# The first stage of a one-core hybrid attention and LRU layer, written in another order

## The chip, the cores and the metric

The kernel runs on one core of one Trainium2 chip. The metric is device time in microseconds (us), the median of repeated runs. Five engines work side by side, each through a queue of its own in order: PE (TensorE, matmuls), DVE (VectorE), ACT (ScalarE), POOL (GpSimd) and SP (SyncE, which here only issues DMAs). An instruction that waits holds back everything behind it on its engine.

## What is computed

A sequence of 512 tokens with 2048 features passes through one layer. The part that matters here is its beginning:

```python
def rms_norm(x, w):
    xf = x.astype(jnp.float32)
    y = xf * lax.rsqrt(jnp.mean(xf * xf, axis=-1, keepdims=True) + EPS)
    return (y * w.astype(jnp.float32)).astype(x.dtype)
...
    h = rms_norm(x, norm_w)
    proj = jnp.einsum('bsd,de->bse', h, w_in)
    q, k, v, g_attn, xr, g_lru = jnp.split(proj, SPLITS, axis=-1)
    attn_out = attention_group(q, k, v, q_norm_w, k_norm_w)
    lru_out = lru_group(xr, conv_w, conv_b, lru_wa, lru_ba, lru_wx, lru_bx, lru_lambda)
    mixed = jnp.concatenate([rms_norm(attn_out, attn_norm_w) * jax.nn.silu(g_attn),
                             rms_norm(lru_out, lru_norm_w) * jax.nn.silu(g_lru)], axis=-1)
    return x + jnp.einsum('bse,ed->bsd', mixed, w_out)
```

The LRU group takes the 1024 columns xr of the projection, convolves each with four taps along the tokens, and sends the result through block-diagonal gates and a scan. Everything is float32.

## The kernel before

Every float32 product is made of three matmuls: each operand is split into a high part (an fp32r copy) and a low part (the rest), and PE adds high x high, high x low and low x high (`mm3`, L152 to L155). x and w_in are both loaded in eight chunks of 256 features, 512 KB each. A chunk of w_in for 512 columns is one tile `wr`, and `wsplit` (L220) splits each of its two halves: ACT copies it to `wh` (L227), DVE subtracts to get `wl` (L228). There are four buffers of `wh` and of `wl` at this time, so a split of a chunk waits until PE has used the chunk two before it; the ring for `wr` holds three chunks.

The first stage computes xr, whose two halves of 512 columns are `a1` (PSUM banks `pj`) and `a2` (banks `mm`). x must arrive transposed. Chunks 0 and 1 are turned on PE (`xturn`, L257). Chunks 2 to 7 are turned by way of DRAM: DVE transposes 32x32 blocks (`block_x`, L345, instructions at L290), SP writes the result to a DRAM tile `xd` in four DMAs (`aside_x`, L350, issued at L305), SP reads it back in one DMA as `xu` (`back_x`, L353, issued at L312), ACT multiplies by norm_w (L360) and copies the high part (L366), and DVE subtracts the low part (L367; the two together are `whole_x`, L356). The read back waits for all four writes.

Beside that, 1/rms is needed: the sums of squares of every chunk (`square_x`, L342: on DVE for chunks 0 and 1, L281; on ACT for the others, L277), their sum on DVE (`xsum`, L401), the power on POOL (`rsqrt_mean`, L371), four small DVE instructions and one of 128x512 that lays the values out on a diagonal (`rows`, L379; L385, L386, L388), a matmul with ones (L395) and a copy to `rbc` (L396). The projection is multiplied by `rbc` as it is taken out of PSUM (`evac_bc`, L502, and L1285 for the first bank).

PE's order is written by hand: chunks 0 and 1 of a1, chunks 0 and 1 of a2, chunks 2 to 7 of a1 with the matmul of L395 ahead of the last quarter of chunk 7, six quarter chunks of a2, and then the gates of LRU block 0 (`lru_pair`, L525, from L553 on), with more of a2 between the gates of the following blocks. Ahead of the gates of a block, DVE takes xr out of PSUM, ACT starts the convolution (`xc`, L535), DVE adds three taps (L540, three times), ACT copies the high part (L545) and DVE subtracts the low part (L546).

What ACT, DVE, SP and POOL do in the first stage, and in which order, is set by the table `moves` (L1244): at the step of PE's order that is its key, it lists what to do. A letter is an action (`acts`, L1239) and the digit a chunk: L loads x, B turns its blocks, D writes them to DRAM, R reads them back, V makes the two parts of x, Q squares; W loads weights of a1 and S splits them; F and P do so for a2; T and H are the turn on PE; C makes some steps of the LRU's constants (`lru_consts`, 16-column instructions on DVE, `lc`); Z is 1/rms. SP and POOL take the first stage's instructions in the written order; for ACT and DVE that holds up to step (6, 0), and from there a scheduler interleaves what is left with the LRU's work. `behind(held)` (L251) tells that scheduler to place an instruction after another one.

Of the kernel before, what the change touches and what calls it, by code (L numbers as in the profile page):

```python
# [63 lines left out]
def hybrid_kernel(  # L64
# [20 lines left out]
    nc = tc.nc  # L85
# [32 lines left out]
    def nm(s):  # L118
        cnt[0] += 1
        return f"{s}_{cnt[0]}"  # L120
# [25 lines left out]
    def const(shape, name, dt=F32):  # L146
        return cp.tile(list(shape), dt, tag=name, name=name)

    def f(ap):
        return ap.bitcast(F32)  # L150
# [55 lines left out]
    loads_done, held = {}, []  # L206

    def wraw(w, r0, c0, nk=1, queue=nc.sync):

        raw = wring.tile([P, 2, SEQ], F32, name=nm("wr"))  # L210
        src = w[r0 : r0 + 2 * P, c0 : c0 + SEQ].rearrange("(k p) e -> p k e", p=P)
        for k in range(nk):
            ks = slice(k * 2 // nk, (k + 1) * 2 // nk)
            with behind(held):
                loads_done[queue] = queue.dma_start(raw[:, ks, :], src[:, ks, :]).ins
            yield raw

# [2 lines left out]
    def wsplit(raw, k, copy=nc.scalar.copy):  # L220

        turn_of[0] += k
        pool = pools["wx" if "wx" in pools and turn_of[0] % 2 else "xw"]
        hi = pool.tile([P, SEQ], F32R, tag="wh", bufs=4, name=nm("wh"))
        lo = pool.tile([P, SEQ], F32R, tag="wl", bufs=4, name=nm("wl"))
        done = (
            copy(hi, raw[:, k, :]).ins,  # L227
            nc.vector.tensor_sub(lo, raw[:, k, :], f(hi)).ins,  # L228
        )
        split_done[-1] = split_done[turn_of[0] - k] = done  # L230
        return hi, lo

# [18 lines left out]
    def behind(those):  # L251
        stack = ExitStack()
        for ins in those:
            stack.enter_context(tc.issue_after(ins))
        return stack
# [71 lines left out]
    chunk, squares, halves, units, reads = {}, {}, {}, {}, []  # L327
# [38 lines left out]
            nc.scalar.copy(hi, v)  # L366
            nc.vector.tensor_sub(lo, v, f(hi))  # L367

    last_pool = [None]

    def rsqrt_mean(dst, src, n, width):  # L371

# [6 lines left out]
    def rows(dst, col, dg):  # L379

        shape = [P, NT, 2, P // 2]
        two = const([P, NT, 4], "two", F32R)[:, :, :2]
        for n in range(2):
            own, other = (slice(m * P // 2, (m + 1) * P // 2) for m in (n, 1 - n))
            nc.vector.tensor_copy(two[own, :, n], col[own])  # L385
            nc.vector.tensor_sub(two[other, :, n], col[own], f(two[own, :, n]))  # L386
        d = dg()
        nc.vector.tensor_mul(  # L388
            d.rearrange("p t (h q) -> p t h q", h=2),
            both_.rearrange("p (h q) -> p h q", h=2)[:, None].broadcast_to(shape),  # L390
            f(two)[:, :, :, None].broadcast_to(shape),
        )
        yield
        pb = pj()
        nc.tensor.matmul(pb, ones_r, d.rearrange("p t q -> p (t q)"), start=True, stop=True)  # L395
        nc.vector.tensor_copy(dst, pb)  # L396
        yield
# [480 lines left out]
    P1, Q6, Q5, Q7, P2, Q3, Q4 = 0, 5, 4, 3, 2, 6, 1  # L878
# [324 lines left out]
    with tc.high_priority():  # L1203
        xs, ws = xload(0, 2), wraw(w_in, 0, C_XR, 2)
        nc.scalar.dma_start(nw_st, norm_w.rearrange("(k p) -> k p", p=P))
        xc, raw = next(xs), next(ws)
# [28 lines left out]
    def vectors(_):  # L1235
# [6 lines left out]
        "C": lambda n: drain(itertools.islice(lrc, n)), "F": fetch_next, "P": split_next, "G": vectors,  # L1242
    }
    moves = {  # L1244
# [10 lines left out]
    }  # L1255

    def move(step):
# [5 lines left out]
    done = []  # L1263
# [22 lines left out]

    s1.close()
    s0.close()
    held.append(reads[-1])
    last_x = loads_done["lru"] = reads[-1]  # L1290
    wsums = itertools.chain(first_sums(), more_sums())

# [209 lines left out]
```

## Time and profile before

| | us |
|---|---|
| median of 3 runs | 628.86 |
| lowest, highest run | 628.76, 628.90 |
| profiled execution, device time | 629.26 |
| its span, first to last instruction | 627.3 |
| outside the span (the difference) | 1.96 |
| mean granted TensorE clock | 1.00 |

A row of a timeline shows the start and the duration in us, the engine and line, output and inputs, and in brackets the idle time of the engine before it with what ended it. "x2" is two instructions in one row; the duration is then that of both.

### The profile page before, as it was taken

How to read it: one execution, taken by the hardware profiler on the slowest of the kernel's cores; microseconds unless marked ns; L12 is line 12 of the kernel's file. 1: busy time of each engine (PE TensorE's matmuls, PEld its weight loads, DVE VectorE, ACT ScalarE, POOL GpSimd, SP SyncE). 2: the span in 40 equal slices, each digit the busy share in tenths (PEclk: the TensorE clock that was granted, in tenths of full speed). 3: DMA queues.
4: the chain of work that ended last, by engine and by line, in shares of the span. 5: the costliest groups of instructions: out<-in, count | busy, mean ns of one | idle time of the engine just before them, and what ended most of it. 6: DMA issues, size and time to landing. Idle time of an engine off the chain costs nothing.

```text
span 627.3 us, 8287 instructions
## 1 busy us (share of the span) xinstructions
PE 620.0 (99%) x2732; PEld 509.4 (81%) x2732; DVE 495.8 (79%) x789; ACT 360.8 (58%) x648; POOL 106.2 (17%) x142
## 2 busy tenths in 40 slices
PE   9999999999999999999999999999999999999997
PEld 7787788887888788888888888888888888888886
DVE  6577878997979896787787888549979866887776
ACT  4587589869946832645485547338346534433441
POOL 3001111112003442521123232100210101010010
PEclk9999999999999999999999999999999999999999
DMA  8996989557975589688669646932995776897262
GB/s 287 358 296 219 262 149 240 142 140 172 245 224 165 164 185 246 133 191 274 187 193 271 194 126 187 279 90 69 262 266 176 234 244 226 300 334 238 68 202 100
DMA packets 76218, 130.76 MB, mean 208 GB/s; under 512 B 6952, under 2 KB 31120, under 8 KB 76176
## 3 DMA queue, kind: packets, MB, share of 16 engines
q1 hardware_dynamic: 68064, 112.75, 57.6%
q0 software_dynamic: 7936, 17.36, 14.7%
q8 instruction: 21, 0.34, 0.2%
q14 instruction: 21, 0.17, 0.1%
q10 hardware_dynamic: 176, 0.14, 0.1%
HBM read 111.87 MB, written 39.32 MB: 241 GB/s over the span
## 4 chain that ended last, share of the span: by engine, by line
PE 79%; DVE 9%; DMA 5%; ACT 4%; issue 2%; SPq 1%; POOL 1%; DVEq 0%; ACTq 0%
PE pj L155 14%; PE pj L153 14%; PE pj L154 14%; PE mm L1065 14%; PE pj L1065 11%; PE mm L155 4%; PE mm L153 4%; PE mm L154 4%; DMA wr<-in_w_in_dram 2%; DVE wl L228 2%; DVE b L584 1%; DMA xu<-xd 1%; ACT wh L227 1%; DVE k L540 1%; DVE b L581 1%
## 5 line engine op out<-in xcount | busy, mean ns | idle before, releaser
L227 ACT CAST wh<-wr 128x512 fp32r<-128x512 f32 x142 | 84.3, 617 | 79.6 <-PE pj L154 32.0
L155 PE MATMUL pj<-x,wl 128*128 128x512 f32 x304 | 118.6, 390 | 0.6 <-DVE wl L228 0.6
L153 PE MATMUL pj<-x,wh 128*128 128x512 f32 x304 | 118.5, 390 | 0.6 <-ACT wh L227 0.6
L154 PE MATMUL pj<-x,wh 128*128 128x512 f32 x304 | 118.3, 389 | 0.0
L228 DVE TENSOR_TENSOR wl<-wr,wh 128x512 fp32r<-128x512 f32 x144 | 98.8, 713 | 17.7 <-ACT wh L227 16.3
L913 ACT CAST wh<-wr 128x1024 fp32r<-128x1024 f32 (+1 forms) x72 | 60.6, 860 | 75.2 <-PE mm L1065 35.4
L914 DVE TENSOR_TENSOR wl<-wr,wh 128x1024 fp32r<-128x1024 f32 (+1 forms) x72 | 68.5, 983 | 29.1 <-ACT wh L913 29.0
L154 PE MATMUL pj<-wl,x 128*128 128x512 f32 x192 | 75.0, 390 | 0.5 <-DVE wl L228 0.5
L153 PE MATMUL pj<-wh,x 128*128 128x512 f32 x192 | 74.9, 390 | 0.2 <-ACT ev L627 0.2
L155 PE MATMUL pj<-wh,x 128*128 128x512 f32 x192 | 74.8, 389 | 0.0
L155 PEld LDWEIGHTS pj<-x,wl 128*128 128x128 f32 x304 | 57.1, 188 | 13.8 <-DVE wl L228 1.9
L153 PEld LDWEIGHTS pj<-x,wh 128*128 128x128 f32 x304 | 57.1, 188 | 12.7 <-ACT wh L227 1.3
L154 PEld LDWEIGHTS pj<-x,wh 128*128 128x128 f32 x304 | 57.1, 188 | 11.8
L937 POOL DMA_DIRECT2D t<-in_w_out_dram x40 | 33.3, 896 | 137.8 <-DMA t<-in_w_out_dram 76.2
L1065 PE MATMUL mm<-wh,ml 128*128 128x512 f32 x126 | 49.0, 389 | 0.0
L1065 PE MATMUL mm<-wh,mh 128*128 128x512 f32 x126 | 49.0, 389 | 0.0
L1065 PE MATMUL mm<-wl,mh 128*128 128x512 f32 x126 | 49.0, 389 | 0.0
L154 PEld LDWEIGHTS pj<-wl,x 128*128 128x128 f32 x192 | 36.0, 188 | 8.6 <-DVE wl L228 1.2
L153 PEld LDWEIGHTS pj<-wh,x 128*128 128x128 f32 x192 | 36.0, 188 | 8.5 <-ACT ev L627 0.8
L155 PEld LDWEIGHTS pj<-wh,x 128*128 128x128 f32 x192 | 36.0, 188 | 7.4
L737 POOL TENSOR_SCALAR p<-p,sm 128x512 f32<-128x512 f32 x32 | 24.2, 759 | 89.8 <-DVE sm L736 89.8
L1065 PE MATMUL pj<-wl,mh 128*128 128x512 f32 (+1 forms) x100 | 38.5, 385 | 0.0
(229 smaller groups left out, 1171.9 us busy)
## 6 DMA issues: line engine op xcount, KB each, us to landing
wr<-in_w_in_dram SPq DMA_DIRECT2D x71, 512.0 KB, 5.1
wr<-in_w_out_dram SPq DMA_DIRECT2D x21, 512.0 KB, 5.9
t<-in_w_out_dram POOLq DMA_DIRECT2D x40, 256.0 KB, 7.4
wr<-t SPq DMA_DIRECT2D x40, 256.0 KB, 5.4
pd<-u SPq DMA_DIRECT2D x16, 512.0 KB, 3.0
pt<-pd SPq DMA_DIRECT2D x64, 128.0 KB, 3.9
t<-in_w_out_dram SPq DMA_DIRECT2D x24, 256.0 KB, 5.6
wr<-in_w_out_dram SPq DMA_DIRECT2D x22, 256.0 KB, 5.0
```

The lines of the kernel that those rows point to most:

```text
L153: nc.tensor.matmul(acc, lh, rh, start=start, stop=False)
L154: nc.tensor.matmul(acc, lh, rl, start=False, stop=False)
L155: nc.tensor.matmul(acc, ll, rh, start=False, stop=stop)
L227: copy(hi, raw[:, k, :]).ins,
L228: nc.vector.tensor_sub(lo, raw[:, k, :], f(hi)).ins,
L540: nc.vector.scalar_tensor_tensor(xc[:, d0:d1], xr[:, d0 + o : d1 + o], v1(R_CW + j * NB + n), xc[:, d0:d1], op0=ALU.mult, op1=ALU.add,)
L581: nc.vector.tensor_mul(i, i, t)
L737: last_pool[0] = nc.gpsimd.tensor_scalar(p, p, sm, 0.0, op0=ALU.mult, op1=ALU.add).ins
L913: nc.scalar.copy(hi[:, to], b)
L914: nc.vector.tensor_sub(lo[:, to], b, f(hi[:, to]))
L937: nc.gpsimd.dma_start(dst, src, accum_op=ALU.add)
L1065: nc.tensor.matmul(dst[s][:, es], lh[:, ts_], rh[:, es], start=i == ends_[0] and j == 0, stop=i == ends_[1] and j == 2,)
```

## The change

Only the first stage and one condition behind it are touched. The table `moves` is written in another order, and two small edits change what waits in the scheduler's order: the load of a later chunk of weights is placed after the last read back alone, and the split of such a chunk after the diagonal of 1/rms (`laid`).

```diff
-            with behind(held):
+            with behind(held[:1]):
                 loads_done[queue] = queue.dma_start(raw[:, ks, :], src[:, ks, :]).ins
...
-        done = (
-            copy(hi, raw[:, k, :]).ins,
-            nc.vector.tensor_sub(lo, raw[:, k, :], f(hi)).ins,
-        )
+        with behind(held[1:]):
+            done = (
+                copy(hi, raw[:, k, :]).ins,
+                nc.vector.tensor_sub(lo, raw[:, k, :], f(hi)).ins,
+            )
...
-        nc.vector.tensor_mul(
+        laid[0] = nc.vector.tensor_mul(
...
-        None: "G0 Q0 L1 W1 S1 L2 F0 L3 L4 F1 W2",
-        (0, 2): "T1 H1 H1 B2 D2 P0 B3 L5 D3 W3",
+        None: "G0 Q0 L1 W1 S1 L2 F0 L3",
+        (0, 2): "T1 H1 B2 H1 L4 D2 F1 W2 R2",
...
-        (6, 0): "V7 S7 Z0 Z0",
+        (6, 0): "V7 S7 Q7 Q4 Z0 Z0 C3",
...
-    held.append(reads[-1])
+    held.extend((reads[-1], laid[0]))
```

All lines from 226 on stand one line further down in the changed kernel. PE's order is the same in both.

On SP, at the beginning of the stage, this stands in the kernel before. `b4` is a chunk of x, `wr` one of weights, `xd` the write to DRAM and `xu` the read back.

```order
L248 DMA b4_28_219<-in_x_dram 128x4x256
L215 DMA wr_29_221<-in_w_in_dram 128x2x512
L215 DMA wr_30_223<-in_w_in_dram 128x2x512
L305 DMA xd_39_263<-xu_37_257 32x4x256 x4
L248 DMA b4_46_282<-in_x_dram 128x4x256
L305 DMA xd_47_284<-xu_44_276 32x4x256 x4
L215 DMA wr_48_289<-in_w_in_dram 128x2x512
L312 DMA xu_38_258<-xd_39_263 128x1024
```

And at the same place in the changed kernel:

```order
L249 DMA b4_36_257<-in_x_dram 128x4x256
L306 DMA xd_37_259<-xu_34_249 32x4x256 x4
L215 DMA wr_38_264<-in_w_in_dram 128x2x512
L215 DMA wr_39_266<-in_w_in_dram 128x2x512
L313 DMA xu_35_250<-xd_37_259 128x1024
L306 DMA xd_46_295<-xu_44_289 32x4x256 x4
```

The four writes of chunk 2 stand ahead of two chunks of weights, and its read back ahead of the load of chunk 5 and the writes of chunk 3.

On DVE, behind the diagonal of 1/rms, this stands before. `k2_124` is the diagonal, `ev` xr out of PSUM, `wl` a low part of weights.

```order
L388 TENSOR_TENSOR k2_124_725<-both_95,two_720 128x512
L396 COPY rbc_105<-pj_126_766 128x512
L502 TENSOR_TENSOR ev_131_789<-pj_11_169,rbc_105 128x512
L228 TENSOR_TENSOR wl_151_858<-wr_149_855,wh_150_857 128x512
L228 TENSOR_TENSOR wl_153_862<-wr_149_855,wh_152_861 128x512
L502 TENSOR_TENSOR ev_132_791<-pj_12_170,rbc_105 128x512
L1285 TENSOR_TENSOR ev_125_752<-ev_125_752,rbc_105 128x512
```

And in the changed kernel, where `lc` are the LRU's constants of 16 columns:

```order
L389 TENSOR_TENSOR k2_124_714<-both_95,two_709 128x512
L482 TENSOR_TENSOR lc4_567<-lc4_567,lc3_566 128x16
L229 TENSOR_TENSOR wl_146_824<-wr_144_821,wh_145_823 128x512
L483 TENSOR_SCALAR lc4_567<-lc4_567 128x16
L229 TENSOR_TENSOR wl_148_828<-wr_144_821,wh_147_827 128x512
L482 TENSOR_TENSOR lc4_567<-lc4_567,lc3_566 128x16
L397 COPY rbc_105<-pj_126_766 128x512
L483 TENSOR_SCALAR lc4_567<-lc4_567 128x16
L229 TENSOR_TENSOR wl_151_858<-wr_149_855,wh_150_857 128x512
L482 TENSOR_TENSOR lc4_567<-lc4_567,lc3_566 128x16
L229 TENSOR_TENSOR wl_153_862<-wr_149_855,wh_152_861 128x512
L483 TENSOR_SCALAR lc4_567<-lc4_567 128x16
```

The two splits of weights that stood ahead of the diagonal (`wl_146`, `wl_148`) now stand behind it, and the rest of the constants stands between the wide instructions. Up to `ev_125` there follow `k2_135`, `ev_131` and `ev_132` with five more `lc` and constants among them: nine wide and eleven small instructions from the diagonal to `ev_125`, where there were six wide ones.

On ACT, between the splits of two later chunks of weights, this stands before. `k2_136` is the beginning of the convolution of LRU block 0 (from `ev_125`), `k2_137` its high part.

```order
L227 CAST wh_150_857<-wr_149_855 128x512
L227 CAST wh_152_861<-wr_149_855 128x512
L530 CAST k2_134_795<-k2_127_777 128x512
L535 ACTIVATE k2_136_799<-ev_125_752,vec_102 128x512
L227 CAST wh_161_914<-wr_160_912 128x512
L227 CAST wh_163_918<-wr_160_912 128x512
L545 CAST k2_137_804<-k2_136_799 128x512
```

And in the changed kernel:

```order
L228 CAST wh_150_857<-wr_149_855 128x512
L228 CAST wh_152_861<-wr_149_855 128x512
L531 CAST k2_134_795<-k2_127_777 128x512
L228 CAST wh_161_914<-wr_160_912 128x512
L536 ACTIVATE k2_136_799<-ev_125_752,vec_102 128x512
L228 CAST wh_163_918<-wr_160_912 128x512
L546 CAST k2_137_804<-k2_136_799 128x512
```

The beginning of the convolution stands behind the first split of chunk 4 of a2 (`wh_161`) and no longer ahead of it. DVE's three taps stand behind the low part of the same split (`wl_162`) in the changed kernel, where two of the three stood ahead of it.

More of the change, by code (lines that the diff above doesn't have):

```diff
@@ L367, in whole_x @@
             nc.vector.tensor_sub(lo, v, f(hi))
-    last_pool = [None]
+    last_pool, laid = [None], [None]
     def rsqrt_mean(dst, src, n, width):
@@ L391, in rows @@
             f(two)[:, :, :, None].broadcast_to(shape),
-        )
+        ).ins
         yield
```

14 rows, old and new, of the table moves are left out of this document.

## The prediction

> **What bounds the kernel now.** The page comes first: PE is busy all along.
>
> ```profile
> span 627.3 us, 8287 instructions
> PE 620.0 (99%) x2732; PEld 509.4 (81%) x2732; DVE 495.8 (79%) x789; ACT 360.8 (58%) x648; POOL 106.2 (17%) x142
> ```
>
> 620.0 / 2732 is 0.227 us for a matmul. PE's order is not changed, so only its waits can go or come. PE's timeline over the first stage shows them: where a start follows the one before by more than 0.23 us, PE waited.
>
> ```profile
> 18.76 0.48 PE L153 MATMUL mm<-x,wh 128*128 128x512 f32 x1
> ...
> 29.54 0.39 PE L155 MATMUL mm<-x,wl 128*128 128x512 f32 x1
> 30.55 0.50 PE L153 MATMUL pj<-x,wh 128*128 128x512 f32 x1 [0.62 <-ACT wh L227]
> ...
> 64.46 0.47 PE L395 MATMUL pj<-k,ones_r 128*128 128x512 f32 x1 [0.76 <-DVE k L388]
> ...
> 74.54 0.40 PE L154 MATMUL pj<-k,k 128*128 128x512 f32 x1
> ```
>
> The windows view counts the matmuls between the first of these rows and L395 (the second row serves further down):
>
> ```profile
> 18.70:64.40 45.70, 43.80 (x188) 34.45 (x186) 30.04 (x85) 32.27 (x89) 1.60 (x2) 1.00 0.86 282
> 20.00:40.00 20.00, 19.22 (x84) 15.27 (x83) 12.90 (x34) 15.15 (x45) 0.00 (x0) 1.00 1.00 333
> ```
>
> 188 records touch the window; two began before it. 186 × 0.227 = 42.2 us out of 45.7: without a wait L395 would start at 61.0, so PE waits 3.5 us here: 0.8 at chunk 2 (29.54 to 30.55 less a matmul), 0.76 idle at the diagonal, the rest in short waits between them, which all end with the later one. L395 to the low-part gate matmul (74.54) is 10.08 us, 44 matmuls without a wait.
>
> **The path to chunk 2.** The chain of waits shows the path through DRAM, DVE's timeline what stood ahead of it, ACT's its landing.
>
> ```profile
> 15.13 0.34 SPq L305
> 16.00 3.44 DMA xd<-xu
> 20.60 6.99 DMA xu<-xd
> ```
>
> ```profile
> 11.11 1.29 DVE L228 TENSOR_TENSOR wl<-wr,wh 128x512 fp32r<-128x512 f32 x2 [0.26 <-ACT wh L227]
> ...
> 35.21 1.42 DVE L290 STREAM_TRANSPOSE xu<-b 128x256 f32<-128x256 f32 x4
> ```
>
> ```profile
> 27.61 1.34 ACT L360 ACTIVATE xu<-xu,nw 128x512 f32<-128x512 f32 x2 [4.85 <-DMA xu<-xd]
> 30.93 1.33 ACT L360 ACTIVATE xu<-xu,nw 128x512 f32<-128x512 f32 x2
> 43.54 1.34 ACT L360 ACTIVATE xu<-xu,nw 128x512 f32<-128x512 f32 x2 [2.68 <-DMA xu<-xd]
> ```
>
> The writes land at 19.4, yet the read is issued at 20.60, because on SP it stands behind the load of chunk 5, the writes of chunk 3 and a load of weights. In the new order it stands right behind its writes and two loads of weights. The blocks of chunk 2 now follow the first pair of low parts, which ends at 12.4, so writes and read go out 1.3 to 2 us sooner: read issued about 18.8. With 7.0 us for the landing as here, chunk 2 is there at 25.8; PE's first matmul of it came 2.94 us behind ACT's start (30.55 − 27.61), so 28.7, ahead of the 29.77 at which PE is free. The 0.8 us go. If DMA were no faster for it, nothing would go here, but what follows hangs on chunk 5 and not on this.
>
> **The path to L395: chunk 5 and the squares.** ACT has squares last now, so from chunk 5's landing on it works in one piece. How soon it lands: on SP its read stands behind the four writes of chunk 6, in both orders; these wait for the blocks of chunk 6 on DVE, and these stand behind chunk 3's parts, 4.28 us behind their start on ACT (35.21 − 30.93).
>
> ```profile
> 36.66 1.82 SPq L305 DMA_DIRECT2D xd<-xu  x4
> 38.53 0.46 SPq L312 DMA_DIRECT2D xu<-xd  x1
> ```
>
> ```profile
> DMA to landing us min/median/max: 5.0/5.8/7.0
> ```
>
> The last row is the source view of L312. Chunk 3's parts stood right behind chunk 2's (30.93 − 27.61 = 3.3); with chunk 2 at 25.8 they could start at 29.1, and I take 29.5, since chunk 3's read now waits for its own writes right ahead of it on SP. The same steps then give blocks from 33.8 to 35.2, writes of 1.82 and the read of chunk 5 at 37.1 instead of 38.53; with the shortest landing, which that read itself took (38.53 to 43.54), chunk 5 is there at T5 = 42.1. The bounds are 41.2 (chunk 3's parts at 29.1 and 0.5 us of the writes beside the blocks) and 43.5 (no gain). From T5 on:
>
> ```profile
> 49.97 1.32 ACT L360 ACTIVATE xu<-xu,nw 128x512 f32<-128x512 f32 x2
> ...
> 53.27 0.41 ACT L277 ACTIVATE b<-b 128x256 f32<-128x256 f32 x1
> ...
> 54.88 1.32 ACT L360 ACTIVATE xu<-xu,nw 128x512 f32<-128x512 f32 x2
> ```
>
> A chunk's parts with the split of its weights take 3.30 us of ACT (49.97 to 53.27), its squares 1.61 (53.27 to 54.88). Three of the first (chunks 5, 6, 7) and four of the second (5, 6, 7, 4) are 9.9 + 6.44, and with 0.1 for the last to reach DVE the sum `xsum` stands at T5 + 16.4.
>
> ```profile
> 60.24 0.18 DVE L401 TENSOR_REDUCE xsum<-ssq 128x4 f32<-128x32 f32 x1
> 60.34 0.68 DVE L228 TENSOR_TENSOR wl<-wr,wh 128x512 fp32r<-128x512 f32 x1
> 62.24 0.17 DVE L385 CAST two<-rstd 64x4 fp32r<-64x4 f32 x1 [1.22 <-POOL rstd L374]
> 62.32 0.69 DVE L228 TENSOR_TENSOR wl<-wr,wh 128x512 fp32r<-128x512 f32 x1
> 63.05 0.16 DVE L386 TENSOR_TENSOR two<-rstd,two 64x4 fp32r<-64x4 f32 x1
> 63.62 0.69 DVE L388 TENSOR_TENSOR k<-both,two 128x512 fp32r<-128x512 f32 x1
> ```
>
> From `xsum` POOL's power takes 2.00 us (60.24 to 62.24), which nothing shortens. From the first `two` to the diagonal are 1.38 us, of which the low part at 62.32, now behind the diagonal, held 0.6: 0.78 remain. L395 follows the diagonal's start by 0.84. The sum is T5 + 16.4 + 2.00 + 0.78 + 0.84 = T5 + 20.0, so 62.2: 2.3 us sooner than 64.46, with 1.2 us of wait left of the 3.5.
>
> **What the change adds: the gates.** Low parts and constants that stood ahead of the diagonal now stand behind it, and so ahead of `ev_125`; and on ACT the beginning of the convolution (L535) now stands behind the split `wh_161`.
>
> ```profile
> 69.91 1.53 DVE L540 SCALAR_TENSOR_TENSOR k<-ev,vec,k 128x510 f32<-128x510 f32 x2
> 71.58 0.69 DVE L228 TENSOR_TENSOR wl<-wr,wh 128x512 fp32r<-128x512 f32 x1
> 72.19 0.75 DVE L540 SCALAR_TENSOR_TENSOR k<-ev,vec,k 128x511 f32<-128x511 f32 x1
> ...
> 73.68 0.69 DVE L546 TENSOR_TENSOR k<-k,k 128x512 fp32r<-128x512 f32 x1
> ```
>
> ```profile
> 68.82 0.82 ACT L535 ACTIVATE k<-ev,vec 128x512 f32<-128x512 f32 x1 [0.38 <-DVE ev L1285]
> ...
> 70.93 1.31 ACT L227 CAST wh<-wr 128x512 fp32r<-128x512 f32 x2 [1.29 <-PE mm L154]
> ...
> 73.03 0.62 ACT L545 CAST k<-k 128x512 fp32r<-128x512 f32 x1 [0.79 <-DVE k L540]
> ```
>
> `wh_161` waits for PE to release its buffer, and does so 6.47 us behind L395 (70.93 − 64.46) in PE's unchanged order. Before, L535 had gone ahead of that wait, at 68.82; now it and everything behind it wait: from L395 on 6.47, `wh_161` 0.66 (half of 1.31), L535 0.82, a tap 0.77 (half of 1.53), `wl_164` 0.61 (71.58 to 72.19), two taps 0.77 + 0.75, high part 0.62, low part 0.69: 12.2 us to the end of the low part, and some 0.1 to PE. Before, PE was there after 10.08. So PE gets a new wait of about 2.2 us in front of the second gate matmul, at 62.2 + 12.3 = 74.5, which is when it was there before (74.54).
>
> The prices of the instructions that now stand behind the diagonal on DVE are in these rows:
>
> ```profile
> 53.05 1.28 DVE L228 TENSOR_TENSOR wl<-wr,wh 128x512 fp32r<-128x512 f32 x2
> 54.25 0.17 DVE L481 TENSOR_TENSOR lc<-lc,lc 128x16 f32<-128x16 f32 x1
> ```
>
> The small one starts 1.20 behind the first of two wide ones, so a wide one costs 0.60; a small one lets the next begin 0.10 later (60.24 to 60.34). Nine wide instructions at 0.60 and eleven small ones at 0.10 from the diagonal on end `ev_125` 6.5 + 0.7 us behind its start, 6.4 behind L395 and ahead of `wh_161`'s end, so they cost nothing under this cover. Were `wh_161` free sooner, they would be next: `ev_125` would then hold L535 to within 0.7 us of the same time.
>
> **The sum.** Waits ahead of L395 less 2.3 us, wait at the gates 2.2 more: −0.1 us. PE's later waits, each where DVE's low part is late, I leave as they are:
>
> ```profile
> 142.99 0.50 PE L154 MATMUL pj<-wl,x 128*128 128x512 f32 x1 [0.28 <-DVE wl L228]
> ...
> 149.00 0.50 PE L154 MATMUL pj<-wl,x 128*128 128x512 f32 x1 [0.23 <-DVE wl L228]
> ```
>
> The profiled execution took 629.26 us, 1.96 outside the span and 0.4 above the median of 628.86; −0.1 gives 629.1 there and 628.7 as median. The low end: T5 at 41.2 brings −0.9 more, and 73.3 at the gates is the floor that 61.0 for L395 allows (61.0 + 12.3), so −1.2. A measurement of this kernel can tell about 0.2%, 1.26 us, from no change.
>
> **Rivals.**
> *Slower by the squares' new place.* All of them now stand behind chunk 5, 6 and 7 on ACT, 6.44 us in one piece between the last parts and `xsum`, so each microsecond that chunk 5 lands late goes through to L395 and the gates one for one. It makes the kernel slower from T5 = 42.3 on, and by over 0.2% from 43.5 on. For it: the window of 20 to 40 us above has a DMA share of 1.00, and the new order puts more reads back in front of loads into this window, where one took 6.99 us instead of 5.0. T5 at 44.1 (37.1 + 7.0) gives 2.0 on the forecast: 630.7. Against it: the read issued at 38.53 had the 5.0. Chance 0.16.
>
> *Slower by the number of small instructions.* If each of the eleven costs as much as the one behind the wide row at 62.32 (it begins 0.73 behind that row, 0.13 more than 0.60, and takes 0.16 of its own: 0.29 instead of 0.10), `ev_125` ends 11 × 0.19 = 2.1 us later, 8.5 behind L395. That is past the end of `wh_161` (6.47 + 0.66 = 7.1), and the wait at the gates grows by 1.4: 630.1. The rows at 54.25 and 60.34 speak against it. Chance 0.08. The Trainium skill, in "VectorE: DVE Perf Modes", section "The DRAIN you can't avoid", has it that VectorE empties its pipe after each instruction before the next begins, and so that one should write fewer of them: by that rule this rival would be the likely one. The trace does not bear it out as it stands, since the rows at 54.25 and 60.34 begin 0.08 us before the one ahead has ended.
>
> *Faster.* Chunk 5 lands at 41.2 or sooner, since loads no longer stand ahead of the reads on SP, and the gates come at their floor: −1.2, 627.6. If the low parts at 142 and 149 come sooner as well, because DVE has the constants behind it, their idle 0.28 and 0.23 go too: 627.1. For it: the late read at 20.60 was SP's queue alone. Against it: the DMA share. Chance 0.26.
>
> **How the numbers follow.** The forecast has the remaining 0.50, with 628.7. Faster by over 0.2% (below 627.6): 0.24 of the faster rival and 0.04 of the forecast (T5 at 41.2 alone gives 627.8, so it takes a term besides), 0.28. Slower (above 630.1): 0.14 of the squares, 0.04 of the small ones, 0.04 of the forecast's upper end (T5 = 43.5 is +1.3), 0.22. Within: 0.50. The range 627.0 to 630.4 holds T5 from the floor to 43.8.
>
> **What would show it.** Right: PE has no wait at 29.8; L395 starts near 62.2; a wait of some 2 us appears between the first and the second gate matmul, with ACT's `wh_161` ahead of L535; the gates begin near 74.5. T5 is the start of the first L361 of chunk 5. Wrong: no wait at the gates although L395 came early (another thing released `wh_161`), or the rows of `lc` behind the diagonal fill the time to `ev_125` beyond `wh_161`, or T5 lies past 43.

## The result, and the profile after

| | kernel before | changed kernel |
|---|---|---|
| median of 4 executions each, us | 628.81 | 633.03 |
| lowest, highest | 627.61, 628.90 | 632.15, 633.41 |
| ratio, 95% interval | | 1.007 (1.0052 to 1.0087) |
| profiled execution, device time | 629.26 | 633.15 |
| its span | 627.3 | 631.4 |
| its mean granted TensorE clock | 1.00 | 0.995 |
| timed again later: median (32 and 12 executions) | 629.02 | 630.91 (629.02 to 632.44) |
| ratio then | | 1.003 (1.0017 to 1.0044) |

The forecast was 628.7 with a range of 627.0 to 630.4. The changed kernel is slower, and beyond the range in both measurements. The two measurements of it differ by 2 us, which is itself a part of the answer.

The page of the changed kernel, to be set beside the two lines of before:

```profile
span 631.4 us, 8289 instructions
PE 622.8 (99%) x2732; PEld 511.8 (81%) x2732; DVE 495.5 (78%) x789; ACT 360.8 (57%) x648; POOL 106.0 (17%) x142
```

DVE, ACT and POOL are busy as long as before. PE has the same 2732 matmuls and is busy 2.8 us longer: its matmuls themselves have become slower somewhere. PE's timeline shows where:

```profile
29.45 0.39 PE L155 MATMUL mm<-x,wl 128*128 128x512 f32 x1
29.67 0.39 PE L153 MATMUL pj<-x,wh 128*128 128x512 f32 x1
...
61.77 0.39 PE L155 MATMUL pj<-x,wl 128*128 128x512 f32 x1
64.29 0.47 PE L396 MATMUL pj<-k,ones_r 128*128 128x512 f32 x1 [2.13 <-DVE lc L482]
64.59 0.40 PE L153 MATMUL pj<-x,wh 128*128 128x512 f32 x1
64.82 0.58 PE L154 MATMUL pj<-x,wh 128*128 128x512 f32 x1
65.21 0.63 PE L155 MATMUL pj<-x,wl 128*128 128x512 f32 x1
65.63 0.63 PE L153 MATMUL pj<-x,wh 128*128 128x512 f32 x1
...
75.50 0.39 PE L155 MATMUL mm<-x,wl 128*128 128x512 f32 x1
77.23 0.51 PE L153 MATMUL pj<-k,k 128*128 128x512 f32 x1 [1.34 <-ACT k L546]
77.96 0.50 PE L154 MATMUL pj<-k,k 128*128 128x512 f32 x1 [0.22 <-DVE k L547]
...
78.53 0.62 PE L153 MATMUL pj<-k,k 128*128 128x512 f32 x1
78.95 0.63 PE L154 MATMUL pj<-k,k 128*128 128x512 f32 x1
```

At 29.67 chunk 2 is there without a wait: that part went as planned. But the waits of the stage now stand together ahead of the diagonal's matmul (L396, which was L395): 2.29 us in one piece beyond a matmul's 0.23. The gates wait 1.50 and 0.50 us more. And behind each of the two waits the starts are 0.43 us apart instead of 0.23. The windows view, cut at the edges of these stretches, has the time in which PE was busy behind the comma, and the granted clock in the third column from the end:

```profile
61.45:64.86 3.41, 1.28 (x7) 0.76 (x6) 2.07 (x9) 1.05 (x3) 2.06 (x3) 1.00 1.01 290
64.86:68.28 3.42, 3.42 (x10) 2.65 (x9) 3.00 (x10) 1.76 (x3) 0.83 (x1) 0.50 0.95 222
...
75.10:78.52 3.42, 1.86 (x7) 1.00 (x6) 2.65 (x5) 1.94 (x4) 1.68 (x2) 1.00 0.61 165
78.52:81.93 3.41, 3.41 (x9) 2.64 (x8) 2.58 (x4) 3.40 (x5) 0.00 (x0) 0.50 0.89 122
```

Two stretches of 3.4 us have a clock of 0.50. Each follows a stretch in which PE was busy for only 1.28 or 1.86 us of 3.4. In 3.4 us PE starts 8 matmuls at 0.43 where it would start 15, so each stretch costs about 1.6 us. I call such a stretch a fall of the clock. A fall takes 3.4 × 0.5 / 631 = 0.0027 off the mean clock of an execution, so that 0.997 is one fall and 0.995 two; the four executions of the first measurement have 0.995, 0.997, 0.997 and 0.995, and all four lie above 632. The two with one fall (633.41, 632.15) are not clearly shorter than the two with two (633.15, 632.91).

The sum against before: L396 starts 0.17 us sooner than L395 did (64.29, 64.46). The second gate matmul starts 3.42 us later (77.96, 74.54), of which 1.5 is the first fall and 2.0 the waits at the gates. The second fall adds 1.7: the matmul that started at 76.82 starts at 81.94. That is 5.1; the span grew by 4.1, so 1.0 came back further down, where PE had waited at 142.99, 149.00 and 209 before.

Why L396 came no sooner is in ACT's timeline (parts of chunks 2, 3, 5, 6, 7), DVE's and SP's:

```profile
24.39 1.34 ACT L361 ACTIVATE xu<-xu,nw 128x512 f32<-128x512 f32 x2 [2.72 <-DMA xu<-xd]
30.13 1.34 ACT L361 ACTIVATE xu<-xu,nw 128x512 f32<-128x512 f32 x2 [2.34 <-DMA xu<-xd]
...
43.05 1.34 ACT L361 ACTIVATE xu<-xu,nw 128x512 f32<-128x512 f32 x2 [0.36 <-DMA xu<-xd]
...
48.77 1.34 ACT L361 ACTIVATE xu<-xu,nw 128x512 f32<-128x512 f32 x2 [0.70 <-DMA xu<-xd]
...
54.37 1.34 ACT L361 ACTIVATE xu<-xu,nw 128x512 f32<-128x512 f32 x2 [0.58 <-DMA xu<-xd]
```

```profile
35.14 1.42 DVE L291 STREAM_TRANSPOSE xu<-b 128x256 f32<-128x256 f32 x4 [0.64 <-DMA b<-in_x_dram]
...
61.03 0.19 DVE L402 TENSOR_REDUCE xsum<-ssq 128x4 f32<-128x32 f32 x1 [2.28 <-ACT b L278]
62.68 0.16 DVE L386 CAST two<-rstd 64x4 fp32r<-64x4 f32 x1 [1.46 <-POOL rstd L375]
```

```profile
28.95 0.33 SPq L313 DMA_DIRECT2D xu<-xd  x1
29.33 0.43 SPq L249 DMA_DIRECT2D b<-in_x_dram  x1
...
36.59 1.88 SPq L306 DMA_DIRECT2D xd<-xu  x4
38.57 0.41 SPq L313 DMA_DIRECT2D xu<-xd  x1
```

Chunk 2 is there 3.2 us sooner than before (24.39, 27.61) and chunk 5 only 0.5 (43.05, 43.54). The load of chunk 6 (29.33) now stands on SP behind a read back that waits for its writes until 28.95; DVE's blocks of chunk 6 wait for that load and start at 35.14, where they started at 35.21 before. Its writes stand ahead of the read back of chunk 5, so this went out at 38.57 (38.53 before). Chunks 6 and 7 then land 0.70 and 0.58 us late for ACT, and the squares behind them end with `xsum` at 61.03, 0.8 later than before.

### The profile page after: what moved, and what is told of

It reads as the page before. It is cut to its first block, busy times and chain, and to the rows that moved or that the text cites. A ratio compares the mean times of both kernels' runs of the same rounds, so it can differ in the third digit from the quotient of the medians.

```text
span 631.4 us, 8289 instructions
## 1 busy us (share of the span) xinstructions
PE 622.8 (99%) x2732; PEld 511.8 (81%) x2732; DVE 495.5 (78%) x789; ACT 360.8 (57%) x648; POOL 106.0 (17%) x142
## 4 chain that ended last, share of the span: by engine, by line
PE 83%; DVE 7%; DMA 6%; ACT 2%; issue 1%; SPq 1%; POOL 0%; ACTq 0%; DVEq 0%
PE pj L154 16%; PE pj L155 15%; PE pj L153 15%; PE mm L1066 14%; PE pj L1066 11%; PE mm L154 4%; PE mm L153 4%; PE mm L155 4%; DMA wr<-in_w_in_dram 2%; DMA xu<-xd 2%; DVE wl L229 1%; DMA xd<-xu 1%; DVE k L541 1%; DVE xu L291 1%; DVE b L585 1%
```

## The experiments

Two theories on the slow matmuls. C: a fall of the clock is a cost by itself, caused by PE's waits. O: it only stands beside work of ACT and DVE that sets the end. Two on the gates: W, `wh_161` ahead of the convolution; R, the load on DVE behind the diagonal. Three on L396: Q, the squares at the end; T, the reads back; L, the load of chunk 6. Every kernel was timed beside the first kernel on the same chip, in up to 12 executions (medians and ratios below; the first kernel's own median was 629.1 beside the first four kernels, 629.02 beside the next four and 628.71 beside the last four). "Without a fall" means a mean clock of 0.999 or 1.000; the 0.999 comes from the end, where the clock falls behind the last matmul (for the last 1.8 us of one profile). The mean clock of an execution says that it had a fall, not where.

### Filling the wait at the gates

```diff
                     pg = bank()
+                    for _ in range(6 if n == j0 == d == 0 else 0):
+                        nc.tensor.matmul(pg, ones_r, xh[KT - 1], start=True, stop=True)
                     mm3(pg, gh[:, j0 + d, :], gl[:, j0 + d, :], ch, cl, True, True)
```

> The changed kernel with six matmuls put into PE's wait ahead of the first gate matmul; their result is overwritten by that matmul, and no other engine's order changes. In the changed kernel PE waits there 1.50 and 0.50 us, and the matmuls behind it start 0.43 us apart, instead of 0.23, for 3.4 us. Theory C (a wait of about 1.5 us and more lets the granted clock fall to a half for 3.4 us, and this is a cost by itself): the six end before the gates are ready, the wait that is left is under 0.4 us, the spacing of 0.43 behind the gates goes, and about 1.5 us with it: 631.5. Rival O (the slow matmuls only stand beside work of ACT and DVE that sets the end anyway): 633.0, no change.

Measured: 629.9 (628.5 to 633.19), ratio 1.0015 (1.0001 to 1.003). Ten executions are without a fall, mean 629.7; the two with one are at 632.62 and 633.19. In the profiled execution there is no fall behind the gates, as C expected. The fall behind L396 was missing too, although PE had waited 1.95 us there: a wait of that length can do without. Beside the changed kernel timed again (630.91, below) the six matmuls gain 1.0 us, beside its first measurement 3.1.

### Filling the wait at the diagonal

```diff
         pb = pj()
+        for _ in range(4):
+            nc.tensor.matmul(pb, ones_r, xh[KT - 1], start=True, stop=True)
         nc.tensor.matmul(pb, ones_r, d.rearrange("p t q -> p (t q)"), start=True, stop=True)
```

> The changed kernel with four matmuls (0.9 us) put into PE's wait of 2.29 us ahead of L396; their result is overwritten by L396. ACT's order is the same, on DVE a few instructions behind the diagonal stand in another order. Theory C: if a wait of the 1.4 us left does not let the clock fall, the 0.43 spacing behind L396 goes, `wh_161` starts 6.5 us behind L396 instead of 8.0, the gates come 1.4 us sooner (76.5) and the kernel is at 631.6; the wait at the gates grows to about 2.1 us and the clock still falls there. If 1.4 us is enough for the clock to fall, nothing changes (633.0), which gives the bound from the other side. Rival O: `wh_161` comes 8.0 us behind L396 in any case, 633.0.

Measured: 630.55 (628.9 to 632.52), ratio 1.0018 (1.0004 to 1.0032); four of 12 executions have a fall, and they are 1.5 us longer (means 631.4 and 629.9). No fall behind L396 in the profiled execution, but one behind the gates, where PE had waited 1.50 and 0.50 us:

```profile
72.63:76.05 3.42, 1.85 (x7) 0.99 (x7) 2.65 (x5) 1.85 (x3) 0.95 (x2) 1.00 0.93 314
76.05:79.46 3.41, 3.41 (x10) 2.65 (x9) 2.58 (x5) 3.38 (x6) 0.73 (x1) 0.50 0.78 95
```

Here, too, a stretch with PE busy for 1.85 of 3.42 us is followed by half the clock.

### The splits not held behind the diagonal

```diff
-        with behind(held[1:]):
-            done = (
+        done = (
```

> The changed kernel without the hold of the splits behind the diagonal: two low parts stand ahead of it on DVE again, and the beginning of the convolution of LRU block 0 stands ahead of `wh_161` on ACT. Theory W (the gates are late because that beginning waits behind `wh_161`, which PE releases): from L396 to the second gate matmul about 12 us instead of 13.7, no wait over 1 us at the gates, so no fall of the clock there; L396 itself up to 0.6 us later, its wait and the fall of the clock behind it stay: 630.6. Rival R (DVE has too much behind the diagonal, in whichever order): the wait at the gates stays within 0.3 us of 2.0: 633.

Measured: 635.87 (633.45 to 637.42), ratio 1.0105: the other way. Without the hold the scheduler put a load of weights on SP ahead of the LRU's gate weights. SP stood at it until 65.15, and the gate weights were issued behind it, the second half of block 0's at 66.10. ACT waited for them:

```profile
65.15 0.39 SPq L215 DMA_DIRECT2D wr<-in_w_in_dram  x1
65.59 0.46 SPq L514 DMA_DIRECT2D k<-in_lru_wa_dram  x1
66.10 0.61 SPq L514 DMA_DIRECT2D k<-in_lru_wx_dram  x1
```

```profile
73.89 0.62 ACT L530 CAST k<-k 128x512 fp32r<-128x512 f32 x1 [4.98 <-DMA k<-in_lru_wx_dram]
```

Every execution has a fall or more (clock 0.992 to 0.997). So this kernel says nothing on W or R; it shows that the hold on ACT and DVE also set SP's order.

### The squares of chunk 4 earlier

```diff
-        (4, 0): "C2 V5 S5 Q5 W7 R7",
+        (4, 0): "Q4 C2 V5 S5 Q5 W7 R7",
...
-        (6, 0): "V7 S7 Q7 Q4 Z0 Z0 C3",
+        (6, 0): "V7 S7 Q7 Z0 Z0 C3",
```

> The changed kernel with one word moved: the squares of chunk 4 are made ahead of chunk 5's parts, where ACT waits 2.4 us for data, and not last. Theory Q (squares last set L396): `xsum` and L396 come 1.6 us sooner, L396 near 62.7 with a wait of 0.7 instead of 2.3 us, so the clock does not fall behind it, another 1.4: the gates near 75.0 instead of 78.0, 630.0. Rival T (the last chunk's read back sets L396): `xsum` moves by under 0.5 us, and the time by under 1 us: 632.5.

Measured: 628.69 (627.54 to 630.19), ratio 0.9995 (0.9984 to 1.0005): one word takes back the whole loss. Eleven of 12 executions are without a fall, mean 628.6. In the profiled execution:

```profile
60.08 0.19 DVE L402 TENSOR_REDUCE xsum<-ssq 128x4 f32<-128x32 f32 x1 [0.67 <-ACT b L278]
```

```profile
63.69 0.40 PE L396 MATMUL pj<-k,ones_r 128*128 128x512 f32 x1
```

`xsum` stood 5.0 us behind the start of chunk 7's parts (60.08 and 55.04), where the changed kernel needed 6.7 (61.03 and 54.37): that is Q's 1.6. The reads landed later than in the profile of the changed kernel (chunk 5 at 45.21), so `xsum` itself came 0.95 sooner: Q and T both hold. The wait ahead of L396 was gone, and with it the fall. Not all of the gain is the squares': the scheduler now put the beginning of the convolution ahead of `wh_161`, and the second gate matmul stood 11.5 us behind L396 (12.1 in the changed kernel without a fall, next).

### The changed kernel again

> The changed kernel as it is, timed again beside the others. Theory C (waits of PE let the clock fall, and whether one does depends on how it lies): every execution has a mean clock below 0.999, some with one fall (0.997) and some with two (0.995), and those with two are about 1.5 us longer than those with one. Rival O: time and mean clock are not related; 632.2 to 633.4 as before.

Measured: 630.91 (629.02 to 632.44), ratio 1.003. Eight executions are without a fall, 629.02 to 631.33, mean 630.2; four have one, 631.54 to 632.44, mean 631.9. So the expectation that every execution falls was wrong, and the 1.7 us between the groups is what C expects of a fall. The profiled execution had none, with these waits:

```profile
61.88 0.39 PE L155 MATMUL pj<-x,wl 128*128 128x512 f32 x1
63.37 0.47 PE L396 MATMUL pj<-k,ones_r 128*128 128x512 f32 x1 [1.10 <-DVE lc L482]
...
72.99 0.39 PE L155 MATMUL mm<-x,wl 128*128 128x512 f32 x1
74.72 0.50 PE L153 MATMUL pj<-k,k 128*128 128x512 f32 x1 [1.34 <-ACT k L546]
75.45 0.50 PE L154 MATMUL pj<-k,k 128*128 128x512 f32 x1 [0.23 <-DVE k L547]
```

Its span is 627.3, that of the first kernel: the second gate matmul is 0.9 us later than there, and all of it came back by 211 us. This is the fastest of the 12, so no profile shows where the other executions without a fall lose their time. The same 1.50 and 0.50 us at the gates that let the clock fall in other profiles did not here.

### The beginning of the convolution pinned ahead of `wh_161`

```diff
-        with behind(held[1:]):
+        with behind(held[1:] + (taps if (turn_of[0], k) in ((12, 0), (13, 1)) else [])):
...
-                nc.scalar.activation(
+                start = nc.scalar.activation(
                     xc, xr, AF.Identity, bias=v1(R_CB + n), scale=v1(R_CW + 2 * NB + n)
-                )
+                ).ins
+                if n == 0:
+                    taps.append(start)
...
+                    if n == 0 and j == 1:
+                        taps.append(tap)
```

> The changed kernel with the two splits of chunk 4 of a2 pinned behind the beginning of the convolution (ACT) and its second tap (DVE), nothing else moved. Theory W (the gates wait because `wh_161` stands ahead of the convolution): the wait at the gates falls from 2.0 to under 0.7 us, no fall of the clock there, 630.3. Rival R (the low parts and constants behind the diagonal hold DVE, so `ev_125` is late whoever stands first on ACT): `ev_125` starts 6.0 us behind L396 as in the changed kernel, the low part of the convolution ends about 12.4 behind L396, so with L396 near 64.3 the gates are at 76.7; the wait there stays at 1.0 us or more in executions without a fall behind L396: 631.5.

Measured: 630.54 (629.54 to 632.39), ratio 1.0029 (1.0017 to 1.004), as the changed kernel, and near the 630.3 that W gave. Three executions have a fall (629.54, 630.76, 631.32) and are no longer than the other nine (mean 630.6), which speaks against a fixed price of a fall. In the profiled execution L396 stood at 64.02 and the second gate matmul at 75.94, 11.92 behind it; in the changed kernel without a fall it was 12.08 (63.37, 75.45).

```profile
70.20 0.82 ACT L536 ACTIVATE k<-ev,vec 128x512 f32<-128x512 f32 x1 [3.41 <-DVE ev L1290]
70.92 1.13 ACT L228 CAST wh<-wr 128x512 fp32r<-128x512 f32 x2
```

The beginning of the convolution now waits for DVE's `ev_125` and starts only 6.2 us behind L396, about when PE releases `wh_161`'s buffer. PE still waited 1.38 and 0.50 us at the gates, where W had expected under 0.7. So W alone is wrong and R holds: with DVE's load behind the diagonal, taking away one of the two limits leaves the other 0.2 us behind it.

### The first kernel with the squares of chunk 4 last

```diff
-        (2, 0): "V3 S3 B6 Q1 Q4 R4 W5 L7 D6",
+        (2, 0): "V3 S3 B6 Q1 R4 W5 L7 D6",
...
-        (6, 0): "V7 S7 Z0 Z0",
+        (6, 0): "V7 S7 Q4 Z0 Z0",
```

> The first kernel with one word moved: the squares of chunk 4 are made last, behind chunk 7's. Theory Q with C: L395 comes 1.6 us later (66.1), all of it a wait of PE, 2.5 us in one piece; in most executions the clock falls behind it, which makes another 1.4: median 631.9, and the executions with a mean clock of 0.997 or less are about 1.5 us longer than the others. Rival O: 630.5, in all executions alike.

Measured: 630.82 (630.56 to 632.53; 9 executions), ratio 1.0032 (1.0019 to 1.0046). One word costs the first kernel 1.8 us, but the profiled execution (630.58) does not show it as Q has it:

```profile
59.43 0.18 DVE L401 TENSOR_REDUCE xsum<-ssq 128x4 f32<-128x32 f32 x1
```

```profile
64.02 0.47 PE L395 MATMUL pj<-k,ones_r 128*128 128x512 f32 x1 [1.14 <-DVE k L388]
```

`xsum` did not wait for the squares: it stands behind DVE's low parts of chunk 7, 5.37 us behind the start of chunk 7's parts on ACT, as in the first kernel (5.36). L395 came 0.44 us sooner than there and not 1.6 later. The loss is at the gates: the second gate matmul stands 11.42 us behind L395 (10.08 before), since the scheduler put DVE's instructions behind the diagonal in another order, with `ev_125` two wide instructions later. So that the price of the word is near 1.6 is luck, and this kernel neither bears Q out nor refutes it for the changed kernel. Only three of nine executions have a fall, and they are 0.6 us longer: the wait was 1.30 us and not 2.5 in the profiled execution, and C's share here is small. The median is nearer to O's 630.5 than to 631.9.

### Squares and constants moved

```diff
-        (4, 0): "C2 V5 S5 Q5 W7 R7",
-        (5, 0): "C3 V6 S6 Q6",
-        (6, 0): "V7 S7 Q7 Q4 Z0 Z0 C3",
+        (4, 0): "Q4 C2 V5 S5 Q5 W7 R7",
+        (5, 0): "C6 V6 S6 Q6",
+        (6, 0): "V7 S7 Q7 Z0 Z0",
```

> The changed kernel with two words moved: the squares of chunk 4 ahead of chunk 5's parts, and the last constants ahead of chunk 6's parts instead of behind 1/rms. With that the beginning of the convolution stands ahead of `wh_161` by the scheduler's own choice, and no small instruction stands behind the diagonal. Theory Q with R: L396 near 62.7, `ev_125` starts 5 us behind it instead of 6, second gate matmul 11 us behind L396 (73.7, before 74.5), no wait over 1 us and no fall of the clock: 627.8, 0.2% ahead of the first kernel. Rival T (the reads back set L396, and they scatter by 2 us): like the squares moved alone, 628.7.

Measured: 627.93 (626.27 to 628.95), ratio 0.998 (0.9969 to 0.9992): ahead of both kernels. Ten executions are without a fall, and two have one (628.25, 628.86). In the profiled execution:

```profile
62.67 0.39 PE L155 MATMUL pj<-x,wl 128*128 128x512 f32 x1
63.10 0.47 PE L396 MATMUL pj<-k,ones_r 128*128 128x512 f32 x1
...
73.53 0.49 PE L153 MATMUL pj<-k,k 128*128 128x512 f32 x1 [0.43 <-ACT k L546]
74.26 0.50 PE L154 MATMUL pj<-k,k 128*128 128x512 f32 x1 [0.23 <-DVE k L547]
```

L396 has no wait to speak of, the second gate matmul stands 11.2 behind it, 0.9 less than in the changed kernel without a fall: about what eleven small instructions cost at 0.08 to 0.10 each. ACT's order changed with them (the convolution ahead of `wh_161`), so the two shares aren't told apart.

### Both waits filled

> The changed kernel with both fillings: four matmuls ahead of L396 and six ahead of the first gate matmul, their results overwritten. Theory C: no wait of PE in this part is longer than 1.4 us, so the mean clock is 0.999 or more in nearly every execution, the executions of 631.5 and more go, and what is left is the changed kernel without a fall: 629.7, the mean of its own executions with a clock of 0.999 and more being 630.2. Rival O: as the changed kernel, 630.9 on this chip, a third of the executions above 631.5.

Measured: 629.94 (628.55 to 631.55), ratio 1.0018 (1.0005 to 1.0031). All 12 executions are without a fall. The next kernel, which differs from the changed kernel by the place of one DMA and was timed beside this one, has a fall in seven of 12. So filling PE's waits takes the falls away, and the changed kernel without falls is 1.2 us behind the first kernel.

### The load of chunk 6 ahead

```diff
-        (1, 0, 1): "V2 S2 W3 R4 L6 Q1 B5 D5",
+        (1, 0, 1): "V2 S2 L6 W3 R4 Q1 B5 D5",
```

> The changed kernel with one word moved: the load of chunk 6 of x is issued ahead of a load of weights and of the read back of chunk 4, and not behind them; no other engine's order changes. Theory L (the read back of chunk 5 gained nothing because chunk 6, whose writes stand ahead of it, was loaded 3 us later than before): the load goes out near 26.1 instead of 29.3, the blocks of chunk 6 no longer wait for it and start at 33.9 (35.1), the read back of chunk 5 goes out at 37.3 (38.6) and its parts start at 42 (43.0 to 44.0). Rival N (DMA is full in that stretch, and whatever goes first delays another): chunk 6's blocks come sooner, but chunk 4's read back lands later by as much, and chunk 5's parts start at 43 or later. The time would move by under 1 us either way, since chunks 6 and 7 follow: 630.5.

Measured: 631.87 (629.17 to 634.75), ratio 1.0047 (1.0028 to 1.0067). The load went out at 25.37 instead of 29.33, and yet:

```profile
35.14 1.29 DVE L229 TENSOR_TENSOR wl<-wr,wh 128x512 fp32r<-128x512 f32 x2 [1.47 <-ACT wh L228]
36.35 1.42 DVE L291 STREAM_TRANSPOSE xu<-b 128x256 f32<-128x256 f32 x4
```

DVE's blocks of chunk 6 start at 36.35, 1.2 us later than in the changed kernel, now behind a low part of weights that waits for `wh`, and this for its load on ACT:

```profile
34.49 1.14 ACT L228 CAST wh<-wr 128x512 fp32r<-128x512 f32 x2 [1.62 <-DMA wr<-in_w_in_dram]
```

Chunk 5's parts start at 45.37. L is wrong as a remedy. N holds in its main point, that a transfer that goes first makes another late where DMA is full (a share of 0.98 from 20 to 40 us in the changed kernel). It was not as N had it, though: the weights of chunk 3 were late, not chunk 4's read back, and chunk 6's blocks came no sooner. Seven executions have a fall, mean 633.0; five have none, 630.3.

### Reads back ahead of writes

```diff
-        (1, 0, 1): "V2 S2 W3 R4 L6 Q1 B5 D5",
-        (2, 0): "V3 S3 W4 L7 B6 D6 R5 W5",
-        (3, 0): "V4 Q2 S4 B7 D7 R6 W6",
+        (1, 0, 1): "V2 S2 L6 W3 R4 Q1 B5 D5",
+        (2, 0): "V3 S3 W4 L7 B6 R5 D6 W5",
+        (3, 0): "V4 Q2 S4 B7 R6 D7 W6",
```

(on top of squares and constants moved)

> The kernel of the squares and the constants moved (two words), with three more: the load of chunk 6 ahead as before, the read back of chunk 5 ahead of the writes of chunk 6, and that of chunk 6 ahead of those of chunk 7. Theory T (the reads back set when PE gets chunks 5 to 7, and they stand on SP behind writes that wait for DVE): chunk 5's parts start near 41 instead of 44, PE's waits at 45.6 to 48 (1.9 us) go, chunk 7 sets L396 alone, which starts near 62: 626.7. Rival N: the reads go out 2.5 us sooner and land at the same time: 627.9.

Measured: 627.82 (627.06 to 629.92), ratio 0.9986 (0.9974 to 0.9998), like the kernel with only the two words moved. Chunk 5's parts started at 42.39 instead of 44.06 and PE's wait there went, but chunk 7's started at 54.25 (54.80), so L396 moved by 0.5 (62.56). All 12 executions are without a fall. T holds for chunk 5 and fails for what counts, chunk 7.

### The two small edits alone

```diff
+            with behind(held[:1]):
...
+        with behind(held[1:]):
...
+    held.extend((reads[-1], laid[0]))
```

> The first kernel with the two small edits alone (loads behind the last read back only, splits behind the diagonal), in its own order of the first stage. Theory W (low parts behind the diagonal cost at the gates what they save at L395): L395 0.6 us sooner, two more wide instructions ahead of `ev_125`, the gates within 0.5 us of 74.5: 629.2. Rival: the edits are where the time goes (a later weight split stalls PE further on): a wait of over 1 us behind 80 us, 630.5 or more.

Measured: 629.95 (628.48 to 631.28), ratio 1.0017 (1.0004 to 1.0029). L396 stood at 63.22, without a wait, the second gate matmul at 74.34 (74.54 before). Six executions are without a fall, mean 629.25, and six have one, mean 630.4. As W expected, what is won at L396 (1.24 us) is nearly all lost by the gates. But the edits are not free: they cost 1.2 us in the median, 0.5 of it in executions without a fall (629.25 beside 628.71) and the rest in falls, which the first kernel had in three of 35. That is more than half of the 1.9 that the changed kernel loses when timed again. In the profile PE waited 1.50 us at chunk 2 (30.75); whether the falls of the other executions stand behind that wait isn't shown. The rival's wait behind 80 us did not show. With the squares and constants moved the same two edits stand in a kernel that is faster than the first, so what they cost hangs on the order.

## Why the prediction was wrong

**Chunk 2: right.** No wait at 29.7; the parts start at 24.39 (25.8 expected).

**Chunk 5: the step that failed first.** "These stand behind chunk 3's parts, 4.28 us behind their start" was taken over from the old order. In the first profile chunk 3's parts start at 30.13 and not 29.5 (0.6 late), and the blocks of chunk 6 stand 5.01 behind them and not 4.28 (0.7), since they wait for the load of chunk 6, which the prediction doesn't follow past the read back that SP waits at. The read back went out at 38.57 and not 37.1 and landed in 4.5 us and not 5.0, so T5 was 43.05 and not 42.1. In the profiles of the changed kernel and its fillings it was 43.0 to 44.0; in those where the blocks came by 34.6 without a wait for the load, the read back still went out between 38.0 and 38.3. The load put ahead made it worse, so this was no slip of the order alone. But by the prediction's own price, one for one, T5 of 43.05 gives 629.7, inside its range: this miss alone doesn't explain the time.

**ACT in one piece: half right.** From T5 to `xsum` 16.4 us were expected. In the second profile of the changed kernel (parts of chunk 5 at 43.64, `xsum` at 60.11) it is 16.5. In the first, ACT waits 0.70 and 0.58 us for chunks 6 and 7, and it is 18.0. The sum from `xsum` to L396 was 3.6; it measured 3.26, as POOL's part took 1.65 and not 2.00. "Which nothing shortens" was wrong by that, and to the good. Together L396 stood at 64.29 and 63.37, not 62.2.

**The gates: right.** 12.3 us from L396 to the second gate matmul were expected, and 12.08 measured without a fall. With one it is 13.67, since `wh_161` waits for PE, and PE was at half the clock: it started 8.0 us behind L396, where 6.47 was expected and 6.4 measured without a fall. That `ev_125` would hold the convolution to within 0.7 us of the same time was right too: pinning it ahead gained 0.2.

**The step that put the time outside the range: the clock, which the sum has at nothing.** Every wait of PE was priced at its own length. The prediction moved four short waits into two long ones and called that even. Waits that stand together let the clock fall, and the sum has no term for it. Its size in the first profile: PE falls behind by 1.5 us in the first fall and by 1.7 in the second. From the forecast's 74.5 the second gate matmul is 3.5 us late, 2.1 by L396 and 1.4 by the first fall; the second fall makes it 5.1, and 1.0 came back at 142 to 211, where the forecast had left all as it was. Executions with and without a fall differ by more or less than that: by 1.7 us for the changed kernel, by 1.5 and 3.2 with one wait filled, by nothing with the convolution pinned. When the kernel was timed again, the eight executions without a fall had a mean of 630.2, inside the range, and the four with one 631.9, outside it.

What is left is 1.2 to 1.4 us in executions without a fall (630.2 beside 628.9; 1.0018 with both waits filled). That L396, 1.2 to 2.1 us later than forecast, makes it is likely but not shown: in the one profile of the changed kernel without a fall, the fastest, all of it came back.

**The rivals.** *The squares' new place* was the likeliest story of those given and its direction was right: in the changed kernel `xsum` waits for the squares, and one word put back takes the loss away. Its price was a shift of T5, where the first profile has late reads of chunks 6 and 7 besides, and falls of the clock. *Small instructions* cost 0.08 to 0.10 each, as assumed. By the rule quoted there from the Trainium skill ("VectorE: DVE Perf Modes", section "The DRAIN you can't avoid") they would have cost more. The same section adds that an instruction that is not held starts earlier, and the trace agrees with that: behind the diagonal the next instruction starts 0.08 us behind a small one (64.06 and 64.14). *Faster* failed on chunk 5, but its second half, the waits at 142 and 149, did come down.

**Which waits let the clock fall.** The length of a wait doesn't decide it: 1.50 and 0.50 us at the gates did in three profiles and did not in the second one of the changed kernel; 1.95 us ahead of L396 did not, 2.29 did. The traces answer this. Each keeps a table of the times at which the granted clock changed, and in all 14 profiles these lie whole multiples of 3.413 us apart, from the rise at the start to the fall behind the last matmul: in the first profile of the changed kernel at 6.84, 64.86, 68.28, 78.52, 81.93 and 631.48 us (17, 1, 3, 1 and 161 multiples), in the second at 6.10 and 627.32 (182). So the clock is set over fixed stretches, whose edges don't move with a wait. Cut at these edges, the second profile of the changed kernel shows stretches that were not followed by a fall, and so does that of the two small edits alone (the last row):

```profile
60.71:64.12 3.41, 2.31 (x10) 1.61 (x10) 2.24 (x9) 0.88 (x2) 1.97 (x2) 1.00 1.03 309
...
70.95:74.36 3.41, 2.43 (x11) 1.69 (x9) 2.96 (x5) 0.99 (x3) 0.00 (x0) 1.00 0.95 317
74.36:77.78 3.42, 2.83 (x11) 2.11 (x12) 3.00 (x5) 3.39 (x5) 1.68 (x2) 1.00 0.66 165
```

```profile
29.42:32.83 3.41, 1.92 (x7) 1.31 (x8) 2.50 (x4) 3.41 (x7) 0.00 (x0) 1.00 1.06 369
```

In the second profile an edge (74.36) parts the waits at the gates, so that PE was busy for 2.43 and 2.83 us of the two stretches; in the first, both lie in one stretch, with 1.86. Over all 14 profiles, each of the six stretches inside the kernel with PE busy for 1.86 us or less (0.40, 0.95, 1.28, 1.84, 1.85, 1.86) was followed by half the clock, and none with 1.92 or more was, from the rise at the start to the last matmul; the nearest are 1.92, 1.93 (the 1.95 us ahead of L396) and 1.97. The Trainium skill, "TensorE: Matmul & The Clock Gate", section "What's actually happening", tells of a free-running window of about 3.4 us, and the traces agree with the length and with the edges that stay. The advice of the Trainium skill on the same page, section "HAM oscillation — how this bites in real kernels", that no idle gap of PE be longer than about 3.4 us, is too lax for this kernel: 2.29 us, or 1.50 and 0.50 in one stretch, were enough.

**What stays open.** The limit between 1.86 and 1.92 us is read from the profiles afterwards, by the busy time of this view, whose matmul ends are modelled; no run set a wait against a stretch on purpose. Why all four executions of the first measurement have a fall, and only four of 12 later, isn't known: L396's wait was 2.29 us in the one profile and 1.26 in the other, and the landing of the reads back differs from execution to execution.

## What to carry to other kernels

On a kernel that PE bounds, a sum of PE's waits isn't the cost: waits that gather in one stretch of 3.41 us, so that PE is busy for little over half of it (1.86 us here), halve the clock for the next 3.41 us, and the same waits spread over two stretches don't. Look at the spacing of the matmuls behind a wait and at each execution's mean clock before comparing medians; a few matmuls that wait for nothing, put into the wait, tell the clock's share from the wait's. When an order written by hand is changed, follow every queue entry that now stands behind a waiting one, loads of later chunks above all, and put optional work (squares, constants) where an engine waits anyway and not last. Then look at what a scheduler placed differently behind it: one word moved in the first stage also changed DVE's and ACT's order at the gates.

## What the hardware showed that was not expected

- The clock fell to 0.50 for 3.41 us behind stretches of 3.41 us in which PE was busy for 0.40 to 1.86 us, and behind none with 1.92 or more; the edges of the stretches stayed fixed over a whole execution.
- The same kernel on the same chip has executions with and without a fall (629.02 to 632.44); even the first kernel has one in 7 of 32 executions, 0.7 us longer on average (629.6 and 628.9).
- Loads and reads back trade places where the DMA share is near 1: chunk 6 issued 4.0 us sooner was turned 1.2 us later.
